# Hybrid decoder trunk, two layers on one core: sums and turns moved from TensorE to VectorE and DRAM, some low halves of weights to GpSimd

## The chip, the cores and the metric

The kernel runs on one NeuronCore of one Trainium2 chip. The metric is the device time of one execution in microseconds (us), median of several runs; lower is better. TensorE does the matrix products (in the profile PE, its weight loads PEld), VectorE is DVE, ScalarE is ACT, GpSimd is POOL, and SyncE (SP) issues DMAs. SBUF is the on-chip memory with 128 partitions, PSUM the banks into which TensorE writes, DRAM the memory outside the core.

## The reference

Two layers over a sequence of 512 tokens with 1024 features. One layer, cut to what matters here:

```
hn = rmsnorm(x, pre_g)
proj = hn @ w_in                       # 1024 x 6664
y_ret = retention(q, k, v) * silu(g)   # 4 heads, each head's output normalized over its 128 features
y_ssd = ssd_mixer(...)                 # 2 groups; values x * delta, states, rmsnorm over 256 features of a group
y_sb  = stick_breaking(...) * silu(g)  # 4 heads
y_mem = memory_read(q, rmsnorm(mem)) * silu(g)   # 4 heads
y = concat(y_ret, y_ssd, y_sb, y_mem) @ w_out    # 2048 x 1024
x = x + rmsnorm(y, post_g)
```

All of it is in float32.

## The kernel before, in words

**Products in three parts.** A float32 product is made of three matmuls in a shorter format. Each operand is split into a high half (ScalarE copies it into the short format, `split`, L293) and a low half (VectorE subtracts that copy from the original, L294), and `mm3` adds high times high, high times low and low times high (L287 to L290, all issued by `mm`, L285). Activations `hTh`, `hTl` hold the normalized input with features on partitions; weights `wh`, `wl` are 1024 columns wide and come in "subs".

**Weights.** A layer has 39 blocks of weights, each of two subs. Blocks come from DRAM in order into one of two `raw` buffers by a DMA that ScalarE's queue issues (L353). `w_prefetch` (L312) splits sub after sub into five slots of `wh` and `wl`: the split of sub k+5 can start when TensorE has finished with sub k. When the second sub of a block has been split, its `raw` buffer is free, and the DMA of the block after next is issued.

**Order.** The builder runs the layer once in Python, and a scheduler places each engine's instructions in an order of its own by a timeline; dependences, not the text, set it. Each projection counts as a unit (`tick`), and `defer(n, f)` runs `f` n units later, so that its operands have had time to arrive. A layer goes: memory values and keys, stick-breaking heads, retention heads, two state-space groups, gates, output projection in two halves of 512 columns (`out_proj`). At the layer change the second half's four token chunks (128 tokens each) end one after the other; `post` (L1164) makes the new x, stores it to DRAM, and `prenorm` (L484) normalizes it for the next layer and turns it, so that features lie on partitions: eight transposes of 128x128 on TensorE into PSUM (`transposed`, L479), then `split` into `hTh` and `hTl`. While chunks 1 to 3 end, TensorE already makes the next layer's memory keys and values; `behind` keeps each chunk's transposes after a given product. The next layer's first products of `hTh` are those of `sb_v` (`proj_a`, chunk after chunk, first the first four blocks of 128 features for all chunks, then the last four).

**Squares of a row.** The retention heads and the state-space groups need, for each token, a sum of squares over partitions. VectorE adds partitions 64 to 127 to 0 to 63 (and in the heads 32 to 63 to 0 to 31), the rest is split into high and low in `z`, and one matmul with a matrix of ones (`onesr`, L881 for two heads, L1069 for a group) adds up the partitions. `row_rstd` (L803) copies the resulting row to SBUF (L808), spreads it by DMA over 32 partitions of 16 tokens each (L811), GpSimd adds epsilon and takes the power -1/2 (L812, L813), and the result goes by DMA to DRAM (L815) and back, the same row into all partitions (L818). `scaled` (L886) and `ssd_norm` (L1075) multiply by it.

**State-space values.** `ssd_values` (L994) turns the two convolved tiles of a group by eight TensorE transposes (L1003) into PSUM and multiplies them from there by `delta` (L1007) and by the decay (L1009) for `ssd_states` and `ssd_out`.

**Turns by VectorE and DRAM** are already used for other tiles: `nc.vector.transpose` turns each 32x32 block in its place, four DMAs write the blocks to a buffer in DRAM, each to the place where it belongs (`through_dram`, L650; `columns_turned`, L663), and one DMA reads the turned tile back (L651, L668).

**GpSimd** already makes some low halves, those of the turned attention weights (L675, L759), and masks (L736, L835, L989).

## Time and profile before

| | |
|---|---|
| runs before | 923.71, 925.14, 924.06 us; median 924.06 us |
| profiled execution | 923.25 us; span of its instructions 921.5 us, so 1.75 us lie outside the span |
| mean granted TensorE clock in it | 0.998 |
| busy share: PE, PEld, DVE, ACT, POOL | 99%, 84%, 73%, 48%, 16% |
| instructions | 12952 |

How to read it: a busy share is the time in which at least one instruction of the engine was under way, over the span. Matmuls overlap in the pipeline: the duration of one (about 0.39 us at 512 columns) is longer than the time from its start to the next one's start, and it is the latter that TensorE's time is made of. A row of the timeline gives start, duration, engine, line, operation, tiles and count, and in brackets how long the engine sat idle before it and for whom. A line such as L285 is that of a helper; tiles (`wl`, `hTh`, `pj`, `mx`) say what it worked on. `pj` and `mx` are PSUM banks, `s`, `y`, `r` are SBUF tiles of 512 columns, `turned` and `row` buffers in DRAM.

### The profile page before, as it was taken

Reading aid. Unit: us, or ns where it says so; the run is one execution under the profiler, and the core shown is the slowest. Engines: PE = TensorE matmul, PEld = TensorE weight load, DVE = VectorE, ACT = ScalarE, POOL = GpSimd, SP = SyncE. Lnnn points to the kernel's source line nnn. Section 1 sums busy time; section 2 is a strip of 40 time slices with the busy share of each in tenths; the row PEclk is TensorE's granted clock in tenths of the full one; section 3 lists DMA queues with packets and bytes.
Section 4 is the critical chain, followed back from the end, with each engine's and each line's share of the span. In section 5 each row is a group of like instructions: output and inputs, shape, how many; then the busy total and the mean of one; then the engine's idle time right before and its main releaser. Section 6 shows DMA issues by size and latency. Waiting matters only on the chain.

```text
span 921.5 us, 12952 instructions
## 1 busy us (share of the span) xinstructions
PE 913.2 (99%) x4667; PEld 773.6 (84%) x4667; DVE 673.3 (73%) x1081; ACT 443.5 (48%) x841; POOL 146.3 (16%) x208
## 2 busy tenths in 40 slices
PE   9999999999999999999999999999999999999997
PEld 7998888888888888888899888888888888888885
DVE  6855689888787887844587476898778869687343
ACT  6643485744453342733465336675445434335341
POOL 1200152320131110100040002423112120102001
PEclk9999999999999999999999999999999999999999
DMA  8544664642444333444345256556333362422502
GB/s 316 213 141 144 169 167 104 199 146 61 120 134 148 116 109 126 137 149 158 116 173 196 93 172 183 124 122 183 103 109 116 110 194 92 139 95 88 210 12 91
DMA packets 105408, 128.53 MB, mean 139 GB/s; under 512 B 64640, under 2 KB 79744, under 8 KB 96256
## 3 DMA queue, kind: packets, MB, share of 16 engines
q10 hardware_dynamic: 10224, 73.44, 23.4%
q1 hardware_dynamic: 95120, 54.28, 20.7%
q8 instruction: 36, 0.59, 0.3%
q14 instruction: 28, 0.23, 0.1%
HBM read 112.10 MB, written 15.56 MB: 139 GB/s over the span
## 4 chain that ended last, share of the span: by engine, by line
PE 98%; DMA 1%; ACT 0%; DVEq 0%; SPq 0%; POOLq 0%; issue 0%; POOL 0%; ACTq 0%; DVE 0%
PE pj L285 74%; PE mx L285 23%; PE mx L479 1%; DMA mem<-memT 1%; PE mx L1003 0%; ACT s L523 0%; DVEq L1331 0%; ACT s L1168 0%; POOLq L1331 0%; ACT wh L293 0%; SPq L506 0%; SPq L349 0%; SPq L1206 0%; POOL t L449 0%; ACTq L1331 0%
## 5 line engine op out<-in xcount | busy, mean ns | idle before, releaser
L285 PE MATMUL pj<-hTh,wh 128*128 128x512 f32 x704 | 276.4, 393 | 0.0
L285 PE MATMUL pj<-hTh,wl 128*128 128x512 f32 x704 | 275.8, 392 | 0.0
L285 PE MATMUL pj<-hTl,wh 128*128 128x512 f32 x704 | 274.6, 390 | 0.0
L294 DVE TENSOR_TENSOR wl<-raw,wh 128x1024 fp32r<-128x1024 f32 (+2 forms) x156 | 188.6, 1214 | 116.9 <-ACT wh L293 115.7
L293 ACT CAST wh<-raw 128x1024 fp32r<-128x1024 f32 (+2 forms) x156 | 158.7, 1020 | 205.0 <-PE pj L285 177.5
L285 PEld LDWEIGHTS pj<-hTh,wl 128*128 128x128 f32 x704 | 132.2, 188 | 27.3
L285 PEld LDWEIGHTS pj<-hTh,wh 128*128 128x128 f32 x704 | 132.3, 188 | 27.1 <-DVE s L593 0.8
L285 PEld LDWEIGHTS pj<-hTl,wh 128*128 128x128 f32 x704 | 132.3, 188 | 26.6
L285 PE MATMUL pj<-wh,s 128*128 128x512 f32 x320 | 97.6, 391 | 0.0
L285 PE MATMUL mx<-s,s 128*128 128x256 f32 (+4 forms) x528 | 79.7, 307 | 0.0
L285 PE MATMUL mx<-wh,s 128*128 128x512 f32 x256 | 79.2, 389 | 0.0
L285 PEld LDWEIGHTS mx<-s,s 128*128 128x128 f32 (+1 forms) x528 | 65.8, 177 | 8.2 <-PE pj L285 1.4
L285 PEld LDWEIGHTS pj<-wh,s 128*128 128x128 f32 x320 | 59.7, 188 | 12.4
L285 PE MATMUL pj<-wl,s 128*128 128x512 f32 x160 | 60.2, 389 | 0.0
L285 PEld LDWEIGHTS mx<-wh,s 128*128 128x128 f32 x256 | 48.1, 188 | 10.0
L294 DVE TENSOR_TENSOR s<-y,s 128x512 fp32r<-128x512 f32 x64 | 41.2, 687 | 19.7 <-ACT s L293 14.0
L262 ACT ACTIVATE s<-s 128x128 f32<-128x128 f32 (+3 forms) x96 | 41.8, 478 | 22.3 <-DVE s L733 20.6
L675 POOL TENSOR_TENSOR s<-y,s 128x512 fp32r<-128x512 f32 x16 | 23.7, 1494 | 179.9 <-ACT s L674 179.4
L293 ACT CAST s<-y 128x512 fp32r<-128x512 f32 x64 | 36.6, 617 | 30.8 <-PE mx L285 22.0
L285 PE MATMUL mx<-wl,s 128*128 128x512 f32 x128 | 49.6, 389 | 0.0
L285 PE MATMUL pj<-wl,hTh 128*128 128x256 f32 (+2 forms) x144 | 47.6, 331 | 0.0
L285 PE MATMUL pj<-wh,hTl 128*128 128x256 f32 (+2 forms) x144 | 47.5, 330 | 0.0
(185 smaller groups left out, 1298.5 us busy)
## 6 DMA issues: line engine op xcount, KB each, us to landing
raw<-wts ACTq DMA_DIRECT2D x69, 1024.0 KB, 4.8
s<-x SPq DMA_DIRECT2D x24, 256.0 KB, 4.1
y<-turned SPq DMA_DIRECT2D x24, 256.0 KB, 2.8
turned<-y SPq DMA_DIRECT2D x64, 64.0 KB, 2.2
s<-acs SPq DMA_DIRECT2D x16, 256.0 KB, 6.3
r<-row SPq DMA_DIRECT2D x12, 256.0 KB, 5.0
raw<-wts SPq DMA_DIRECT2D x4, 512.0 KB, 7.5
raw<-wts SPq DMA_DIRECT2D x2, 1024.0 KB, 6.3
```

Of the source, the lines that this page charges most:

```text
L262: i = self.nc.scalar.activation(out, in_, func, **k)
L285: return self.nc.tensor.matmul(out, lhsT, rhs, start=start, stop=stop)
L293: self.nc.scalar.copy(h, src)
L294: self.nc.vector.tensor_sub(l, src, hf)
L479: x = self.nc.tensor.transpose(b[:, P * j:P * j + P], hn[i][:, P * j:P * j + P], self.con("ident", P))
L675: nc.gpsimd.tensor_sub(p.l, x, p.hf)
```

## The change

1. **Row sums.** The retention heads and state-space groups add partitions on VectorE down to 32; `row_rstd` then turns the 32 partitions by VectorE's transpose and sums over what were partitions by a `tensor_reduce`. The split of `z`, the matmul with `onesr`, the copy of the row and the DMA that spread it are gone. Since the 32 partitions now hold every 32nd token, the write of the row to DRAM goes token by token (pieces of one float) where it was 16 tokens at a time. `scaled` comes 6 units after the second head's squares (before: 3, then 7 more); `ssd_var` and `ssd_norm` each come one unit later.
2. **State-space values** are turned by `columns_turned` (VectorE's transpose, eight DMAs to DRAM, two back) straight after the convolution, and `ssd_values`, three units later instead of two, multiplies the read tiles in place.
3. **Layer change.** Chunk 0 of the new x is turned by `turned_far`: two transposes on VectorE, eight DMAs to DRAM, two back, then `split`. Chunks 1 to 3 stay on TensorE.
4. **Low halves.** `low_by_pool(k)` gives every third sub's low half to GpSimd, except in the memory and stick-breaking heads (subs 16 to 33 of a layer) and at the start: 36 of 156.

```diff
     def w_prefetch(self, upto=None, between=()):
...
-                self.split(x, h[:, c], l[:, c], h[:, c].bitcast(F32))
+                nc = self.nc
+                nc.scalar.copy(h[:, c], x)
+                (nc.gpsimd if self.low_by_pool(k) else nc.vector).tensor_sub(l[:, c], x, h[:, c].bitcast(F32))
...
+    def low_by_pool(self, k):
+        return k > 12 and k % 3 == 2 and not 16 <= k % (2 * NBLK) < 34
...
+    def turned_far(self, hn, t):
+        ts = slice(P * t, P * t + P)
+        H, HF, L = v3(self.hTh[:], KC), v3(self.hTh[:].bitcast(F32), KC), v3(self.hTl[:], KC)
+        for i in range(2):
+            T, ks = self.buf(tag=LT), slice(4 * i, 4 * i + 4)
+            self.nc.vector.transpose(T, hn[i])
+            d = self.turned_rows(SEQ, P)
+            dd = d.rearrange("(b m) (a t) -> a m b t", m=BLK, a=P // BLK)
+            x = self.through_dram(T, dd, d.rearrange("(k p) t -> p k t", p=P), v3(self.buf(tag=LL), 4))
+            self.split(x, H[:, ks, ts], L[:, ks, ts], HF[:, ks, ts])
...
     def row_rstd(...):
-        e = self.buf(tag="r")[0:n]
-        nc.scalar.copy(e, rows)
-        c = self.tiny(RJ)[:n * RP]
-        for i in range(n):
-            nc.sync.dma_start(c[RP * i:RP * i + RP], e[i:i + 1].rearrange("o (p j) -> o p j", j=RJ))
+        T, c = self.buf(tag=RT)[:n * RP], self.tiny(RJ)[:n * RP]
+        nc.vector.transpose(T, z)
+        nc.vector.tensor_reduce(out=c, in_=v3(T, RJ), op=ALU.add, axis=AX.X)
...
-        nc.sync.dma_start(d.rearrange("o (p j) -> (o p) j", j=RJ), c)
+        for i in range(n):
+            nc.sync.dma_start(d[i:i + 1].rearrange("o (j p) -> (o p) j", p=RP), c[RP * i:RP * i + RP])
...
     def ret_head2(...):
-        for n in (64, 32):
-            nc.vector.tensor_add(sq[0:n], sq[0:n], sq[n:2 * n])
...
-        nc.scalar.copy(z[r:r + 32], sq[0:32])
-        nc.vector.tensor_sub(z[r + 32:r + 64], sq[0:32], z[r:r + 32].bitcast(F32))
+        nc.vector.tensor_add(sq[0:64], sq[0:64], sq[64:128])
+        nc.vector.tensor_add(z[RP * (h % 2):RP * (h % 2) + RP], sq[0:32], sq[32:64])
...
-        vb = self.mx()[0:2]
-        self.mm(vb, self.onesr[:, 2:4], z[:], True, True)
...
     def ssd_group(...):
+        X["xt"] = [self.buf(tag=TX), self.buf(tag=TX)]
+        self.columns_turned(X["x"], X["xt"])
+        self.defer(VD, self.ssd_values, X)
-        self.defer(2, self.ssd_values, X)
...
     def ssd_values(...):
-            b = self.mx()
-            for c in (2 * i, 2 * i + 1):
-                for j in range(2):
-                    o = 256 * (c % 2) + P * j
-                    nc.tensor.transpose(b[:, o:o + P], X["x"][j][:, P * c:P * c + P], self.con("ident", P))
-            xdt, xds = self.buf(), self.buf()
+            b = xdt = X["xt"][i]
+            xds = self.buf()
...
     def ssd_var(...):
-        z = self.new(512, F32R, "r")
-        nc.scalar.copy(z[0:64], sq[1][0:64])
-        nc.vector.tensor_sub(z[64:128], sq[1][0:64], z[0:64].bitcast(F32))
-        row = self.mx()[0:1]
-        self.mm(row, self.onesr[:, 0:1], z[:], True, True)
-        X["rB"], = self.row_rstd(row, self.eps4[:RP])
+        nc.vector.tensor_add(sq[0][0:32], sq[1][0:32], sq[1][32:64])
+        X["rB"], = self.row_rstd(sq[0][0:32], self.eps4[:RP])
...
     def post(...):
-            self.turn.append(self.prenorm(x, preB, t))
+            self.turn.append((self.turned_far if t < FAR else self.turned)(self.normed(x, preB), t))
```

Here `VD` is 3, `RD` 6, `FAR` 1; `LT`, `LL` and `RT`, `TX` only name the kind of SBUF tile.

**What stands where.** ScalarE at the layer change. `s_4642` and `s_4636` are junk tiles of chunk 3's sum of squares, `y_4729` and `y_4723` memory keys, `raw_4852` and `raw_4846` the block with sub 90, the first after the four narrow subs of the first `proj_a`. Before:

```order
L293 CAST hTh<-mx_4561 128x4x128
L293 CAST wh_4848<-raw_4697 128x528
L462 ACTIVATE s_4642,t_4641<-s_4336 128x512
L462 ACTIVATE s_4643,t_4641<-s_4337 128x512
L293 CAST wh_4854<-raw_4762 128x528
L353 DMA raw_4852<-wts 128x2048
L293 CAST y_4729<-s_4727 128x512
L293 CAST hTh<-mx_4606 128x4x128
L293 CAST hTh<-mx_4613 128x4x128
```

And now, `y_4492` being the second half of chunk 0 that comes back from DRAM:

```order
L470 ACTIVATE s_4637,t_4635<-s_4323 128x512
L330 CAST wh_4842<-raw_4691 128x528
L295 CAST y_4723<-s_4721 128x512
L330 CAST wh_4848<-raw_4756 128x528
L295 CAST hTh<-y_4492 128x4x128
L295 CAST hTh<-mx_4600 128x4x128
L295 CAST y_4788<-s_4786 128x512
L295 CAST hTh<-mx_4607 128x4x128
L330 CAST wh_4852<-raw_4756 128x528
L361 DMA raw_4846<-wts 128x2048
```

The cast of chunk 0's second half now stands ahead of those of chunk 2 (`mx_4600`, `mx_4607`, before `mx_4606`, `mx_4613`), and the DMA of the block with sub 90, which stood ahead of them all, behind them.

SyncE at the layer change, where the new x is stored (`x_4542` is chunk 1's, `x_4594` chunk 2's, `x_4640` chunk 3's). Before:

```order
L1179 DMA x_4542<-s_4329 128x512
L1179 DMA x_4594<-s_4332 128x512
L1179 DMA x_4594<-s_4333 128x512
L1179 DMA x_4640<-s_4336 128x512
L1179 DMA x_4640<-s_4337 128x512
```

Now, with chunk 0's two halves written to `turned_4480` and `turned_4491` and read back:

```order
L1183 DMA x_4536<-s_4315 128x512
L667 DMA turned_4480<-y_4478 32x16x32 x4
L1183 DMA x_4588<-s_4318 128x512
L668 DMA y_4481<-turned_4480 128x4x128
L1183 DMA x_4588<-s_4319 128x512
L667 DMA turned_4491<-y_4489 32x16x32 x4
L1183 DMA x_4634<-s_4322 128x512
L1183 DMA x_4634<-s_4323 128x512
L668 DMA y_4492<-turned_4491 128x4x128
```

The read of chunk 0's first half stands behind a store of chunk 2, and that of its second half behind both stores of chunk 3.

VectorE in the first state-space group of layer 0, around the values. Before (`s_2898` is the second convolved tile, `mx_2964` and `mx_2975` the banks with the turned values):

```order
L943 SCALAR_TENSOR_TENSOR s_2898<-s_2898,s_2897 128x512
L294 TENSOR_TENSOR s_2726<-mx_2905,s_2726 128x128
L294 TENSOR_TENSOR wl_2955<-raw_2681,wh_2954 128x1024
L951 SCALAR_TENSOR_TENSOR s_2960<-s_2960,pj_2929 128x512
L1082 SCALAR_TENSOR_TENSOR y_1316<-y_1316,s_2960 128x512
L1007 TENSOR_TENSOR s_2969<-mx_2964,t_695 128x256 x2
L1009 TENSOR_TENSOR s_2970<-s_2969,t_713 128x256
```

Now (`s_2886` is that convolved tile, `s_2893` and `s_2894` the values read back, `s_3011` the convolution of the tile after it):

```order
L951 SCALAR_TENSOR_TENSOR s_2886<-s_2886,s_2885 128x512
L677 STREAM_TRANSPOSE y_2902<-s_2886 128x512
L894 TENSOR_TENSOR y_2214<-y_2214,r_2579 128x512
L894 TENSOR_TENSOR y_2376<-y_2376,r_2580 128x512
L331 TENSOR_TENSOR wl_2973<-raw_2686,wh_2972 128x1024
L296 TENSOR_TENSOR s_2731<-mx_2912,s_2731 128x128
L959 SCALAR_TENSOR_TENSOR s_2978<-s_2978,pj_2947 128x512
L1084 SCALAR_TENSOR_TENSOR y_1312<-y_1312,s_2978 128x512
L948 SCALAR_TENSOR_TENSOR s_3011<-pj_2982,hp_721,s_3011 128x511
L948 SCALAR_TENSOR_TENSOR s_3011<-pj_2982,hp_721,s_3011 128x510
L1013 TENSOR_TENSOR s_2893<-s_2893,t_691 128x256 x2
```

The multiplications by `delta` (L1013, before L1007) have moved behind the first two steps of the next convolution, and the normalization of retention heads 0 and 1 (L894, before L886) now stands ahead of them.

33 lines of the change are left out of this document (15 added, 18 removed).

## Prediction

> **What bounds the kernel now.** I read the page's busy shares and its chain first, then TensorE's list of waits, then the chain in order of time.
>
> ```profile
> span 921.5 us, 12952 instructions
> PE 913.2 (99%) x4667; PEld 773.6 (84%) x4667; DVE 673.3 (73%) x1081; ACT 443.5 (48%) x841; POOL 146.3 (16%) x208
> PE 98%; DMA 1%; ACT 0%; DVEq 0%; SPq 0%; POOLq 0%; issue 0%; POOL 0%; ACTq 0%; DVE 0%
> ...
> PE mx L285 <- POOL b L197: 1.2, 1, 1.2
> PE pj L285 <- ACT s L523: 1.0, 2, 0.7
> ...
> ACT wh L293 <- PE pj L285: 177.5, 84, 6.1
> 131.83 5.47 PE pj L285 x24
> ```
>
> A busy PE alone would prove little, since matmuls overlap; but the chain that ended last is 98% PE, and PE waited for others 2.2 us in all (1.2 and 1.0, both at the start). So everything that reaches TensorE is there in time, and the span is the sum of TensorE's issue intervals: 24 matmuls of 512 columns take 5.47 us, 0.228 each. The wait of ScalarE's `wh` casts for PE (177.5 us in all) says the same from the other side: a weight's split starts as soon as TensorE lets go of a slot, with four subs still ahead, 4 x 5.47 = 21.9 us where a sub is 24 such matmuls. An instruction less on TensorE is therefore time off the end, unless a new wait appears; an instruction more elsewhere costs nothing until it comes later than its slack.
>
> **What leaves TensorE.** The groups by shape, then three places of TensorE's timeline.
>
> ```profile
> L479 PE MATMUL mx<-consts,s 128*128 128x128 f32 x64 | 8.6, 273 | 0.0
> L1003 PE MATMUL mx<-consts,s 128*128 128x128 f32 x32 | 5.1, 272 | 0.0
> L285 PE MATMUL mx<-r,onesr 128*1 128x512 f32 x4 | 1.6, 398 | 0.0
> L285 PE MATMUL mx<-r,onesr 128*2 128x512 f32 x4 | 1.6, 396 | 0.0
> ...
> 484.80 1.03 PE L479 MATMUL mx<-consts,s 128*128 128x128 f32 x8
> 485.59 0.71 PE L285 MATMUL pj<-wh,s 128*128 128x512 f32 x2
> 486.14 0.39 PE L285 MATMUL pj<-wl,s 128*128 128x512 f32 x1
> ...
> 831.43 0.40 PE L285 MATMUL mx<-r,onesr 128*1 128x512 f32 x1
> 831.67 1.08 PE L285 MATMUL pj<-wh,s 128*128 128x512 f32 x4
> ```
>
> The 32 transposes L1003 go, 8 of the 64 L479 (chunk 0 of the layer change) and the 8 `onesr` matmuls. Their mean durations (272, 396 ns) are not their price, because they overlap with their neighbours. From 484.80 to 486.14 stand eight transposes and two ordinary matmuls: 1.34 - 2 x 0.228 = 0.88 us, 0.11 each. A `onesr` matmul takes 831.67 - 831.43 = 0.24. So 40 x 0.11 + 8 x 0.24 = 4.4 + 1.9 = **6.3 us** leave the stream. No instruction is added to it. The same rows give an uncertainty: after the eight transposes the next two matmuls took 0.55 instead of 0.46, so a switch between shapes costs 0.09. The scheduler regroups small products in the new order; ten switches more or fewer would be 0.9 us either way, and I take none.
>
> **What is added to VectorE and GpSimd.**
>
> ```profile
> L294 DVE TENSOR_TENSOR wl<-raw,wh 128x1024 fp32r<-128x1024 f32 x144 | 180.5, 1257 | 111.5 <-ACT wh L293 110.4
> L745 DVE STREAM_TRANSPOSE s<-s 128x512 f32<-128x512 f32 x8 | 5.5, 689 | 3.3 <-POOL s L736 3.3
> ...
> L294 DVE TENSOR_TENSOR wl<-raw,wh x156: 681/1225/1809, 5.3 to 897.9; 128x1024 fp32r<-128x1024 f32 x144, 128x528 fp32r<-128x528 f32 x8, 128x512 fp32r<-128x512 f32 x4
> L675 POOL TENSOR_TENSOR s<-y,s x16: 1285/1298/2285, 108.6 to 587.9; 128x512 fp32r<-128x512 f32 x16
> 124.30 4.13 POOL L675 TENSOR_TENSOR s<-y,s 128x512 fp32r<-128x512 f32 x2 [0.82 <-ACT s L674]
> 125.47 1.81 DVE L294 TENSOR_TENSOR wl<-raw,wh 128x1024 fp32r<-128x1024 f32 x1
> ...
> raw<-wts ACTq DMA_DIRECT2D x69, 1024.0 KB, 4.8
> ```
>
> VectorE loses 36 low halves (34 of 1024 columns at 1.26, two of 528 at 0.7: 44 us) and gains eighteen transposes and eight reductions, each 0.69 at most (a reduction taken like a transpose of 512 columns): 18 us. The subtractions of `z` that it also loses are not counted. It goes down by some 26 us out of 673 and, being waited for nowhere by TensorE, gives nothing to the time. GpSimd shows no 1024-column low half; two of 512 columns took 2 x 1.29 = 2.6 us alone and 4.1 beside VectorE (row 124.30), so one costs 2.6 to 4.6 us, 36 of them 94 to 166 us on an engine busy 146 of 921. Such a half arrives 2.6 to 4.6 us after its cast instead of about 1.3, out of 21.9 us of lead: nothing, as long as the lead stands. Behind it in GpSimd's queue stand masks and powers, whose readers come units (5.47 us each) later. When it is the second of a block, ScalarE's DMA of a later block waits for it, some 3 us longer than before, ahead of the casts queued there; that block's cast is due three subs (16.4 us) later and the load takes 4.8, so this too stays inside.
>
> The port between the two engines: in row 125.47 a VectorE low half beside GpSimd took 1.81, the longest of 156, against a median of 1.23, so GpSimd's work cost it 0.58 at most. The Trainium skill ("SBUF — State Buffer", Who interferes with whom) says that a VectorE operation with two SBUF inputs and a GpSimd operation that reads SBUF lock one another out for the whole instruction. By that VectorE would stand still for up to 36 x 2.6 = 94 us, an estimate from the GpSimd row; the trace bears out a conflict but not that length, since 1.81 is less than one operation of each. I take 0.58.
>
> **State-space values through DRAM.**
>
> ```profile
> 269.43 0.69 DVE L943 SCALAR_TENSOR_TENSOR s<-s,s 128x512 f32<-128x512 f32 x1 [0.76 <-ACT s L267]
> 273.46 0.76 DVE L1007 TENSOR_TENSOR s<-mx,t 128x256 f32<-128x256 f32 x2 [0.37 <-PE mx L1003]
> 278.48 1.52 DVE L940 SCALAR_TENSOR_TENSOR s<-pj,hp,s 128x511 f32<-128x511 f32 x2
> 298.80 2.35 PE L285 MATMUL mx<-s,s 128*128 128x128 f32 x14
> ...
> L663 SPq DMA_DIRECT2D turned<-y x48: 303/451/1466, 195.5 to 789.5; - x48
> DMA to landing us min/median/max: 1.5/2.9/5.7
> ...
> L651 SPq DMA_DIRECT2D y<-turned x16: 337/338/341, 82.2 to 576.7; - x16
> DMA to landing us min/median/max: 2.6/2.9/5.6
> ```
>
> In the first group the second convolved tile is done at 270.1. Add a transpose (0.7), four issues on SyncE (4 x 0.45 = 1.8), landing 2.9, the read's issue and landing 0.4 + 2.9: 278.8, with the slowest landings 284.3. The multiplications now stand behind two steps of the next convolution, which ran from 278.48 to 280.0. So VectorE waits 0 to about 4 us there, with that convolution and a low half queued behind it; the products that need the values come in the small matmuls that PE reached no earlier than 298.80. Cost taken: nothing; cover: 15 us.
>
> **Row sums.** The gather and the copy go, the transpose and reduction come (1.4 us), the row is written in single floats.
>
> ```profile
> 843.12 0.34 SPq L818 DMA_DIRECT2D r<-row  x1
> 846.60 1.41 DVE L1075 SCALAR_TENSOR_TENSOR y<-y,consts,r 128x512 f32<-128x512 f32 x2 [4.92 <-DMA r<-row]
> 871.80 0.39 PE L285 MATMUL mx<-wh,s 128*128 128x512 f32 x1
> ```
>
> The tightest reader is the last group's normalization: it gave the operands of the last two of sixteen steps of the output projection's first half, which ended at 871.80; a step is 12 x 0.228 = 2.7 us, so they were due at about 866.3 and split by about 849.5 (846.60 + 1.41 and two splits): 17 us of cover. One unit later takes 5.5 of it. A row is now 512 pieces; the nearest row, L663 with 256 pieces, lands after 2.9, at most 5.7, so 6 us more at the slow end. Cost taken: nothing. The Trainium skill ("DMA: Bandwidth & Descriptors", Rules for kernel authors) says that a non-contiguous last dimension becomes one descriptor per element and advises against it; no run here shows such a write yet, and by that rule too the price is latency in that cover.
>
> **The layer change** is where it is narrow.
>
> ```profile
> 471.00:488.00 17.00, 17.00 (x102) 14.85 (x101) 16.13 (x25) 11.39 (x26) 7.75 (x13) 1.00 0.50 177
> 463.83 19.95 SPq L1179 DMA_DIRECT2D x<-s  x8
> 487.96 0.28 PE L285 MATMUL pj<-wh,hTh 128*128 128x264 f32 x1
> 500.67 12.22 PE pj L285 x99
> ```
>
> In the clock of before, the last store of the new x was issued at 483.8; the read of chunk 0's second half now follows it, so it lands at 484.2 + 2.9 = 487.1, at the slow end 489.8. ScalarE casts it, and behind that wait chunk 2's casts and the DMA of the block with sub 90. Three deadlines follow; TensorE comes to each 0.9 us earlier, since chunk 0's transposes are gone.
> - Chunk 2's first half: landing + two casts (0.6 each) + up to two low halves (0.7 each) = 489.7 (slow 492.4). From 487.96 to 500.67 stand 96 matmuls and eight transposes, 0.123 each without the latter; TensorE needs it at 487.96 + 24 x 0.123 + 0.9 - 0.9 = 490.9. Slack 1.2, or a wait of 1.5.
> - Chunk 0's second half: landing + 0.6 + 0.7 = 488.4 (slow 491.1); needed after 48 of the matmuls, 487.96 + 5.9 = 493.9. Slack 5.5 or 2.8.
> - Sub 90: DMA some 3 us after the landing, 490.1; + 4.8 + cast 1.05 + low half 1.3 = 497.2 (slow 499.9); needed at 500.67 - 0.9 = 499.8. Slack 2.6, or 0.1 late.
>
> VectorE was busy 16.13 of 17.00 us from 471 to 488; it gains two transposes (1.4), loses a low half of 1024 and two of 528 columns (2.7), and beside GpSimd may lose 3 x 0.58 = 1.7: 16.5. It fits. Between a cost of 0 and 1.5 us I take 0, from the median landing.
>
> **Sum.** 923.25 - 6.3 = 916.95 for the profiled execution (1.75 us outside the span unchanged). The median of the runs stands 0.81 above it: **917.8 us**, 0.7% faster. A measurement can tell about 0.2% (1.85 us) from no change. Own range of this case: ten switches less (0.9) and the spread of the runs below (0.35) give 916.5; ten switches more and the wait of 1.5 give 920.2.
>
> **Rivals.** For the first, the landings of all DMAs with `turned`.
>
> ```profile
> L748 SPq DMA_DIRECT2D turned<-s x128: 302/449/2547, 128.1 to 637.8; - x128
> ...
> DMA to landing us min/median/max: 1.4/2.4/7.8
> ```
>
> - *The layer change waits.* The read lands later than 5.6 us after its issue: of all DMAs to and from `turned`, one took 7.8. Then (484.2 + 7.8 + 2.6) chunk 2 comes at 494.6, 3.7 us late, and 917.8 + 3.7 = 921.5. For it: narrow slack and a queue of stores ahead; against it: the landing median. 0.12.
> - *The port lock.* By whole-instruction locking, three low halves on GpSimd hold VectorE for 2.6 + 1.3 + 1.3 = 5.2 us in that stretch: 16.13 + 1.4 - 2.7 + 5.2 = 20.0 of 17, chunks 2 and 3 are 3 us late, 920.8. Against: 1.81. This is the rule of the Trainium skill's SBUF page named above. 0.03.
> - *Slower: weights come late.* A low half stands in GpSimd's in-order queue, and for 17 of the 36 the next load, in ScalarE's queue, stands behind it. If such a half were done more than 16.4 - 4.8 + 21.9 - 2.3 = 31 us after its cast, every microsecond beyond costs TensorE 17 us in all: 917.8 + 17 = 935 at 32 us; slower by 0.2% is reached at about 31.5. For it: GpSimd waits there for tiles that come late (masks, powers); against: the longest of its subtractions took 2.3 us, and the lead is ten times that. 0.06.
> - *No change.* TensorE only looks like the pace, and weight loads or ScalarE take over what it gives back: 924.1. Against: waits of 2.2 us. 0.05.
>
> **How the numbers follow.** Forecast 0.74. Faster: 0.74 + 0.12 + 0.03 = 0.89; same: 0.05; slower: 0.06. The range takes the forecast's own and most of the waiting layer change: 916.5 to 920.8.
>
> **What would show it.** After: no L1003-like transposes, 56 left of the others, no `onesr`; PE's waits still about 2 us; the layer's units as long as before. A row "PE pj <- ACT hTh" or "<- DVE hTl" near 485 would be the first rival, VectorE low halves of over 2 us the second, "PE <- POOL wl" the third. I am wrong if the span is above 919 with PE waiting, or if PE waits nowhere and yet less than 5 us are gone.

## The result: slower by 5%, and the profile after

The changed kernel takes 968.87 us (median of 4 runs, 967.91 to 970.29); the kernel before took 923.89 us (4 runs, 923.71 to 925.14) beside it. The ratio is 1.0497 [1.0485, 1.051]. The forecast was 917.8 us with 920.8 as the upper end.

The page of the changed kernel: its span, the busy time of each engine, and the chain that ended last by engine and by line.

```profile
span 968.6 us, 12904 instructions
PE 927.7 (96%) x4619; PEld 780.9 (81%) x4619; DVE 662.9 (68%) x1060; ACT 430.6 (44%) x821; POOL 241.5 (25%) x244
PE 67%; DMA 12%; DVE 11%; ACT 4%; POOL 3%; issue 3%; SPq 1%; DVEq 0%; ACTq 0%; POOLq 0%
PE pj L287 48%; PE mx L287 18%; DMA row<-t 4%; DMA s<-acs 3%; DMA raw<-wts 2%; POOL t L828 2%; DVE wl L331 2%; DMA r<-row 1%; DVE s L1026 1%; ACT wh L330 1%; DVE s L948 1%; DVE s L998 1%; DVE s L296 1%; DVE y L894 1%; ACT s L264 1%
```

The chain was 98% TensorE; now a third of it lies elsewhere, and the lines named are those of the new rows: the row's write (`row<-t`), the power ahead of it (L828), the row's read, and the broadcasts of the state-space sums (`s<-acs`). VectorE's busy time fell by 10.4 us, where the sum had 26. TensorE's own account: it stood idle for 968.6 - 927.7 = 40.9 us instead of 921.5 - 913.2 = 8.3, which is 32.6 more; and it was busy 14.5 us longer although it has 48 instructions less. The granted clock shows why (mean 0.978 after, 0.998 before): added up over stretches of one microsecond, a lower clock took 17.5 us of TensorE's busy time, and none in the kernel before.

Some of the waits of the changed kernel (engine, line, what it waited for: us in total, times, longest):

```profile
DVE y L1077 <- DMA r<-row: 45.0, 4, 13.5
...
DVE s L998 <- DMA s<-acs: 40.3, 4, 12.0
...
PE mx L287 <- DVE s L1039: 9.4, 3, 4.8
...
PE mx L287 <- DMA s<-turned: 7.4, 4, 2.2
PE mx L287 <- ACT s L295: 6.8, 3, 3.9
```

TensorE's own waits add up to some 34 us. Of these 2.3 us stand at the start, as before, and nearly all the others between 262 and 428 us and between 740 and 861 us, in and just behind the state-space groups of the two layers. VectorE waited 85 us in front of two kinds of DMA, in eight waits of 10 to 11 us on average. The kernel before has the same two waits, with 19.1 us in all:

```profile
DVE y L1075 <- DMA r<-row: 13.9, 4, 4.9
...
DVE s L988 <- DMA s<-acs: 5.2, 6, 2.3
```

Everything that VectorE would have done meanwhile (convolutions, the mixing of the decays, low halves) came late, and TensorE then waited for some of that. The first such place, from SyncE's timeline (start, length of the issue, line, what is issued) and VectorE's:

```profile
250.79 0.84 SPq L831 DMA_DIRECT2D row<-t  x2
256.73 0.34 SPq L834 DMA_DIRECT2D r<-row  x1
257.31 0.38 SPq L685 DMA_DIRECT2D s<-turned  x1
...
258.29 2.62 SPq L996 DMA_DIRECT2D s<-acs  x4
```

```profile
253.87 0.69 DVE L1084 SCALAR_TENSOR_TENSOR y<-y,s 128x512 f32<-128x512 f32 x1
266.60 1.40 DVE L998 TENSOR_TENSOR s<-s,t 128x512 f32<-128x512 f32 x2 [12.04 <-DMA s<-acs]
```

SyncE issues in order. The row is written at 250.79, its read waits on SyncE until the write has landed, at 256.73, and behind that read stand a turned read that TensorE needs and the four broadcasts of the first decay. These go out at 258.29, the first lands 8.3 us later, and VectorE does nothing from 254.56 to 266.60. TensorE, for its part, waits 2.2 us for the turned read, until 262.79. The same place in the kernel before:

```profile
250.98 1.84 SPq L986 DMA_DIRECT2D s<-acs  x4
265.47 1.24 SPq L811 DMA_DIRECT2D t<-r  x2
271.21 0.49 SPq L815 DMA_DIRECT2D row<-t  x1
272.95 0.80 SPq L818 DMA_DIRECT2D r<-row  x2
```

There the broadcasts went first and landed after 4.0 to 6.4 us, and the row's write (271.21) was followed by its read 1.7 us later. In the changed kernel the four broadcasts took 8.2 to 8.6 us to land: they now ran beside the row's two reads and a 1 MB load of weights issued at 257.94, and the DMA engines were 90% busy or more from 260 to 266. So several things are new at once: where the row stands in the queue, how long its write takes to land, and what the DMAs behind it share the engines with. The experiments vary the first two. All row writes before, then all after (issues, and us from issue to landing):

```profile
L815 SPq DMA_DIRECT2D row<-t x8: 316/403/493, 271.2 to 840.4; - x8
DMA to landing us min/median/max: 1.7/2.2/5.4
```

```profile
L831 SPq DMA_DIRECT2D row<-t x12: 302/306/496, 250.8 to 887.1; - x12
DMA to landing us min/median/max: 5.8/6.5/7.4
```

Written float by float, the rows take 6.5 us instead of 2.2 to land (medians; in the kernel before, the two rows of a pair of heads went in one DMA). The chain in order of time shows two more places, at a group's norm and at the layer change:

```profile
363.70 1.40 POOL t L828
365.12 6.58 DMA row<-t
371.72 3.53 DMA r<-row
375.94 0.75 DVE y L1077
376.69 2.39 DVE s L1026 x4
...
505.15 4.19 DMA turned<-y
509.49 2.48 DMA y<-turned
```

That the chain passes through the layer change does not make it a loss: TensorE waited nowhere there for more than 0.1 us.

### The profile page after: what moved, and what is told of

The parts are those of the page before. It is cut to its first block, busy times and chain, and to the rows that moved or that the text cites. A ratio compares the mean times of both kernels' runs of the same rounds, so it can differ in the third digit from the quotient of the medians.

```text
span 968.6 us, 12904 instructions
## 1 busy us (share of the span) xinstructions
PE 927.7 (96%) x4619; PEld 780.9 (81%) x4619; DVE 662.9 (68%) x1060; ACT 430.6 (44%) x821; POOL 241.5 (25%) x244
## 2 busy tenths in 40 slices
DMA packets 135009, 133.76 MB, mean 138 GB/s; under 512 B 91168, under 2 KB 109344, under 8 KB 125856
## 4 chain that ended last, share of the span: by engine, by line
PE 67%; DMA 12%; DVE 11%; ACT 4%; POOL 3%; issue 3%; SPq 1%; DVEq 0%; ACTq 0%; POOLq 0%
PE pj L287 48%; PE mx L287 18%; DMA row<-t 4%; DMA s<-acs 3%; DMA raw<-wts 2%; POOL t L828 2%; DVE wl L331 2%; DMA r<-row 1%; DVE s L1026 1%; ACT wh L330 1%; DVE s L948 1%; DVE s L998 1%; DVE s L296 1%; DVE y L894 1%; ACT s L264 1%
## 5 line engine op out<-in xcount | busy, mean ns | idle before, releaser
L287 PE MATMUL pj<-hTl,wh 128*128 128x512 f32 x704 | 277.8, 395 | 0.0
L331 DVE TENSOR_TENSOR wl<-raw,wh 128x1024 fp32r<-128x1024 f32 (+2 forms) x120 | 146.1, 1223 | 82.4 <-ACT wh L330 68.7
L331 POOL TENSOR_TENSOR wl<-raw,wh 128x1024 fp32r<-128x1024 f32 (+1 forms) x36 | 89.4, 2482 | 284.3 <-ACT wh L330 284.2
L287 PEld LDWEIGHTS pj<-hTh,wh 128*128 128x128 f32 x704 | 134.5, 191 | 27.9 <-DVE s L610 0.8
L287 PE MATMUL mx<-s,s 128*128 128x256 f32 (+4 forms) x528 | 91.5, 340 | 24.6 <-DVE s L1039 9.4
L287 PEld LDWEIGHTS mx<-s,s 128*128 128x128 f32 (+1 forms) x528 | 73.0, 196 | 37.7 <-issue 12.5
L296 DVE TENSOR_TENSOR s<-y,s 128x512 fp32r<-128x512 f32 x64 | 48.3, 800 | 19.5 <-ACT s L295 15.8
```

What stands on the lines that cost most here:

```text
L287: return self.nc.tensor.matmul(out, lhsT, rhs, start=start, stop=stop)
L296: self.nc.vector.tensor_sub(l, src, hf)
L331: (nc.gpsimd if self.low_by_pool(k) else nc.vector).tensor_sub(l[:, c], x, h[:, c].bitcast(F32))
```

## The experiments

The theories, as they are named in the expectations: R, the new row sums cost (R1 by the 4-byte pieces of their write, R2 by their earlier place on SyncE); V, the values through DRAM; G, the low halves on GpSimd; Q and D, whether a late row acts through SyncE's queue or through its own readers. Each kernel was timed beside the kernel before; the ratio to it stands with its interval.

**Undoing the row sums, or making them alone.** `e1_rows_as_before` puts back `row_rstd`, `ret_head3`, `onesr` and `ssd_var`'s split of before into the changed kernel.

```diff
+        vb = self.mx()[0:2]
+        self.mm(vb, self.onesr[:, 2:4], z[:], True, True)
...
-            nc.sync.dma_start(d[i:i + 1].rearrange("o (j p) -> (o p) j", p=RP), c[RP * i:RP * i + RP])
+        nc.sync.dma_start(d.rearrange("o (p j) -> (o p) j", j=RJ), c)
```

> The changed kernel with the row sums as they were before (z split into two, one matmul by onesr, gather, row written in pieces of 64 bytes); low halves on GpSimd, values through DRAM, the far turn and the later norms stay. Theory R (the new row sums are what costs: their row write lands 6 to 7 us after its issue, and the reads and broadcasts behind it on SyncE come late): the loss goes and 40 transposes are saved, 923.9 - 4.4 = 919.5 us. Rival V (the values through DRAM or the low halves on GpSimd starve VectorE): it stays above 950 us.

Measured: 951.68 us, 1.0308 [1.0291, 1.0325]. The loss is not gone; V's figure holds. The wait has moved to the values:

```profile
DVE s L1023 <- DMA s<-turned: 29.6, 4, 10.9
```

`e4_rows_alone` makes the opposite kernel: before, with the new `row_rstd`, the new `ret_head2` and `ssd_var`, and nothing else.

```diff
-            self.defer(3, self.ret_head3, h // 2, z, ys)
+            i = h // 2
+            self.defer(RD, self.scaled, ys, self.row_rstd(z, self.con("reps", 2 * RJ, 2 * RP)[:, RJ * i:RJ * i + RJ], 2))
```

> The kernel before with the new row sums alone (turn and reduction on VectorE, write in pieces of 4 bytes, use six units after the squares; group norms at their old distance); no other part of the change. Theory R: it is slow by itself, over 940 us. Rival V: the row sums alone save the eight onesr matmuls, 923.9 - 1.9 = 922 us.

Measured: 957.11 us, 1.0367 [1.0348, 1.0386]. R's figure holds: the row sums alone cost 34 us. With `e1` this says that neither part is innocent, and that their costs don't add up.

**The size of the pieces.** In `e2_rows_in_64b` the last addition stores its sums so that token 16p+j, not 32j+p, ends in row p; the write then has 16 floats in a piece, and the constant is laid out as before.

```diff
-        nc.vector.tensor_add(z[RP * (h % 2):RP * (h % 2) + RP], sq[0:32], sq[32:64])
+        self.add_by_row(z[RP * (h % 2):RP * (h % 2) + RP], sq[0:32], sq[32:64])
...
+    def add_by_row(self, out, a, b):
+        a, b = (x.rearrange("q (p j) -> q p j", j=RJ) for x in (a, b))
+        self.nc.vector.tensor_add(out.rearrange("q (j p) -> q p j", p=RP), a, b)
...
-            nc.sync.dma_start(d[i:i + 1].rearrange("o (j p) -> (o p) j", p=RP), c[RP * i:RP * i + RP])
+            nc.sync.dma_start(d[i:i + 1].rearrange("o (p j) -> (o p) j", j=RJ), c[RP * i:RP * i + RP])
```

> The changed kernel, but token 16p+j instead of 32j+p ends in row p, place j of the reduced tile, because the last addition writes its sums in that order; the row is then written in pieces of 64 bytes instead of 4. Instructions and their number stay. Theory R1 (the size of the pieces): the write lands 1.7 to 3.4 us after its issue instead of 5.9 to 7.0; about 4.4 us less at each of the eight rows, all of which the chain passes through or nearly: 8 x 4.4 = 35 us, about 934 us. Rival R2 (the place in SyncE's queue: the row's write and read stand ahead of the decay's broadcasts, and wait for the power on GpSimd): the landing is shorter but the wait stands, not below 950 us.

Measured: 930.06 us, 1.0075 [1.0046, 1.0103]. R1: 39 of the 45 us are gone, with as many instructions on every engine as in the changed kernel, on SyncE and GpSimd in the same order and on the others in nearly the same. The write, and the two waits:

```profile
L835 SPq DMA_DIRECT2D row<-t x12: 312/318/421, 251.5 to 840.5; - x12
DMA to landing us min/median/max: 1.3/1.4/3.0
```

```profile
DVE y L1081 <- DMA r<-row: 16.3, 4, 5.1
...
DVE s L1002 <- DMA s<-acs: 9.2, 4, 4.5
```

**The place.** `e3_rows_later` keeps the 4-byte pieces and issues the turn, sums, power, write and reads three units later.

```diff
-            self.defer(RD, self.scaled, ys, self.row_rstd(z, self.con("reps", 2 * RJ, 2 * RP)[:, RJ * i:RJ * i + RJ], 2))
+            self.defer(3, self.rows_late, i, z, ys)
...
+        self.defer(7, self.scaled, ys, self.row_rstd(z, self.con("reps", 2 * RJ, 2 * RP)[:, RJ * i:RJ * i + RJ], 2))
```

> The changed kernel, with the turn, reduction, power, write and read of a pair of retention rows issued three units later and their use one unit later, as far from the squares as before; the write is still in pieces of 4 bytes. Theory R2 (the place in the queue): the first decay's broadcasts go ahead of the first pair's write again, so the first of the three places in each layer (about 8 to 10 us) is made good, about 950 us. Theory R1 (the size of the pieces): the writes still land 6 to 7 us after their issue and what stands behind them is only another victim, above 960 us.

Measured: 982.59 us, 1.064 [1.0608, 1.0671]: 14 us slower than the changed kernel, which neither theory had (R1's bound alone holds). The broadcasts' wait fell from 40.3 to 20.6 us, but the values' reads now stand behind the row, and VectorE's wait for them rose from 4.0 to 28.8 us. Moving the row only changed what stands behind it.

The next three kernels, together with `e4`, make a square of piece size and distance on the kernel before, with the row sums alone. `e11_rows64_alone` has 64-byte pieces (the edit of `e2`) at the old distances (the edit of `e3`).

> The kernel before with the new row sums alone, in pieces of 64 bytes and at the old distances (three units, then seven). Theory R1: nothing is late and the eight onesr matmuls are saved, 923.0 - 1.9 = 921.1 us, against 957.1 for the row sums alone in pieces of 4 bytes. Rival: the turn and reduction on VectorE or the removed hop do harm by themselves, over 925 us.

Measured: 920.68 us, 0.9978 [0.9969, 0.9987]: as forecast by R1, and faster than both kernels. `e13_rows4_old_distance` is the same with the write, its constant and the last additions of the change:

```diff
-            nc.sync.dma_start(d[i:i + 1].rearrange("o (p j) -> (o p) j", j=RJ), c[RP * i:RP * i + RP])
+            nc.sync.dma_start(d[i:i + 1].rearrange("o (j p) -> (o p) j", p=RP), c[RP * i:RP * i + RP])
```

> The kernel before with the new row sums alone at the old distances (three units, then seven), the write in pieces of 4 bytes: it differs from the kernel that took 920.7 us in the size of the pieces alone. Theory R1 (the landing of the write): it lands 6.5 us or later instead of 1.4 and the kernel takes over 940 us. Rival P (the distances decide; at the old ones the 5 us more are covered): 921 to 925 us.

Measured: 936.3 us, 1.0145 [1.0128, 1.0161], landing 6.2/7.5/8.5. The bound of 940 was missed, yet the pieces alone cost 15.6 us at the old distances. `e17_rows64_short_alone` takes `e4_rows_alone` and applies the edit of `e2`.

> The kernel before with the new row sums alone, pieces of 64 bytes, at the new distance (write and reads three units earlier on the queues, use six units after the squares). It fills the square of piece size and distance: 957.1 (4 bytes, new distance), 936.3 (4 bytes, old), 920.7 (64 bytes, old). Theory P3 (the two costs add up, and the earlier place also costs with short landings, since the row's write and reads stand ahead of the decay's broadcasts): 928 to 932 us, which is the 7 to 9 us left in the change with pieces of 64 bytes. Rival (the distance matters only where the write lands late): 920 to 922 us.

Measured: 923.35 us, 1.0003 [0.9993, 1.0012]. P3 falls; the rival is right in kind, and its 922 is missed by 1.4 us. The square is:

| row sums alone | old distance | new distance |
|---|---|---|
| pieces of 64 bytes | 920.7 | 923.4 |
| pieces of 4 bytes | 936.3 | 957.1 |

The new distance costs 2.7 us with a short landing and 20.8 with a long one; the pieces cost 15.6 and 33.8. Taken singly they cost 2.7 and 15.6 us, together 36.4: each makes the other dearer. The new distance changes two places at once, since the row's write and reads go out three units earlier on SyncE and the row is used four units earlier on VectorE; the square does not tell these apart. The next two kernels try to.

**Which way the late row acts.** Both kernels keep the 4-byte pieces. `e9_rows_on_gpsimd` issues the row's write and reads from GpSimd's queue, `e10_acs_on_scalar` the broadcasts from ScalarE's.

```diff
-            nc.sync.dma_start(d[i:i + 1].rearrange("o (j p) -> (o p) j", p=RP), c[RP * i:RP * i + RP])
+            nc.gpsimd.dma_start(d[i:i + 1].rearrange("o (j p) -> (o p) j", p=RP), c[RP * i:RP * i + RP])
...
-            nc.sync.dma_start(out[i], d[i:i + 1].to_broadcast([P, SEQ]))
+            nc.gpsimd.dma_start(out[i], d[i:i + 1].to_broadcast([P, SEQ]))
```

> The changed kernel, its rows still written in pieces of 4 bytes, but the row's write and the reads of it issued by GpSimd (which made the power) instead of SyncE. Theory Q (the loss is SyncE's one queue: while it waits for the row's landing, the decay's broadcasts and the reads behind it are not issued): VectorE's waits for those broadcasts (40 us) shrink and the time falls by 20 us or more, below 950 us. Theory D (the row itself comes late to its two readers on VectorE, whichever queue carries it): the landing stays 6 to 7 us and the time stays above 960 us.

Measured: 978.64 us, 1.06 [1.0585, 1.0614], by its time for D. But it isn't a clean test. VectorE's wait for the broadcasts did fall, to 11.1 us, and the wait moved to GpSimd, whose masks then held TensorE:

```profile
POOL r L834 <- DMA row<-t: 33.5, 6, 7.4
...
PE mx L287 <- POOL s L851: 11.7, 4, 5.9
```

```diff
-            nc.sync.dma_start(v3(a, 4), S["rows"][0, r:r + 4].unsqueeze(0).to_broadcast([P, 4, P]))
+            nc.scalar.dma_start(v3(a, 4), S["rows"][0, r:r + 4].unsqueeze(0).to_broadcast([P, 4, P]))
...
-            nc.sync.dma_start(v3(E[64 * j:64 * j + 64], 4), S["rows"][1, r:r + 4].unsqueeze(0).to_broadcast([64, 4, P]))
+            nc.scalar.dma_start(v3(E[64 * j:64 * j + 64], 4), S["rows"][1, r:r + 4].unsqueeze(0).to_broadcast([64, 4, P]))
```

> The changed kernel with rows in pieces of 4 bytes, all still on SyncE, but the broadcasts of the state-space sums (the decay's and the outputs') issued by ScalarE. Theory Q: these broadcasts no longer stand behind the row's landing; of the three places in each layer at which the chain leaves TensorE, the two with a broadcast behind the row go or shrink: below 950 us. Theory D: the waits move to the row's own readers and the time stays above 960 us.

Measured: 955.8 us, 1.0361 [1.0327, 1.0395]: 13 us back, between the two bounds. VectorE's waits for the broadcasts fell from 40.3 to 18.7 us and for the row from 45.0 to 30.2. So part of the loss is what stood behind the row on SyncE, and a wait for the row itself remains. This test is not clean either: ScalarE's `wh` casts now waited 10.7 us for the row's landing, for which they did not wait before, so the 13 us are a net figure.

**The values through DRAM.** `e6_values_alone` adds them alone to the kernel before.

```diff
-        self.defer(2, self.ssd_values, X)
+        X["xt"] = [self.buf(tag="s"), self.buf(tag="s")]
+        self.columns_turned(X["x"], X["xt"])
+        self.defer(3, self.ssd_values, X)
...
-        self.defer(5, self.ssd_var, X)
-        self.defer(9, self.ssd_norm, X)
+        self.defer(6, self.ssd_var, X)
+        self.defer(10, self.ssd_norm, X)
```

> The kernel before with the state-space values through DRAM alone (taken three units after the convolution, group norms one unit later); row sums, low halves and layer change as before. Theory S (values and row hops share SyncE's one queue, so that the values' read is issued late and VectorE stands in front of it): it is slow by itself, 945 to 955 us. Rival G (the loss of the kernel with the old row sums came from the low halves on GpSimd): 32 transposes are saved, 922.9 - 3.5 = 919.4 us.

Measured: 946.44 us, 1.025 [1.0235, 1.0265]. S holds: by themselves they cost 23 us beside the old rows. VectorE waited 17.5 us in front of their reads. In the first group the last of their writes went out at 275.26, just behind the row's two reads (273.97) and a load of weights (272.85), and the values were read at 281.06. `e5_rows64_values_pe` takes `e2` and turns them on TensorE again (`defer(2, self.ssd_values, X)` and the transposes of before).

> The changed kernel with rows written in pieces of 64 bytes and, besides, the state-space values turned on TensorE as before (two units after the convolution); new row sums, low halves on GpSimd and the far turn stay. Theory S (what is left of the loss is VectorE waiting for the values' read, and everything behind it): the loss of 7 us goes, 8 transposes and 8 onesr matmuls stay saved: 922.9 - 0.9 - 1.9 = 920.1 us. Rival R2 (the row's write and read ahead of the decay's broadcasts cost by their place): not below 926 us.

Measured: 932.25 us, 1.0105 [1.0088, 1.0122]. S falls and R2's bound holds: beside the new rows with short landings the values cost nothing (930.06 with them). `e12_rows64_vd5` gives them more time in `e2`:

```diff
-VD = 3
+VD = 5
```

> The changed kernel with rows in pieces of 64 bytes and the state-space values taken five units after the convolution instead of three. Theory S: the wait of VectorE for the values' read (about 5 us in each layer's first group) goes: 923.0 - 6.3 plus what the rows' place still costs, 917 to 924 us. Rival: the wait is not what was left, 928 to 932 us.

Measured: 932.0 us, 1.0091 [1.0077, 1.0105]: the rival's figure. But the edit did not take the wait away: it was 3.5 us in `e2` and is 3.6 here. So this run does not test S; `e5`, where the wait does not exist, does. `e14_rows64_old_distance_all` has all parts, the edit of `e2` and the later rows of `e3`, so that the row's DMAs come between the values' writes.

> All parts of the changed kernel, rows in pieces of 64 bytes and at the old distances (three units, then seven). Theory P2 (the 7 us that are left with pieces of 64 bytes come from the row's write and read standing ahead of the decay's broadcasts): these waits go and it takes 917 to 922 us. Rival V2 (they come from the values through DRAM together with the rows on SyncE): with the row's hops now between the values' writes and their read as in the kernel with the old rows, it takes over 935 us.

Measured: 939.5 us, 1.0186 [1.0171, 1.02]: V2. Its SyncE timeline, and the landings of the values' writes issued from 268 to 271 and from 275.9 to 276.5:

```profile
268.53 1.96 SPq L680 DMA_DIRECT2D turned<-y  x4
272.71 0.79 SPq L835 DMA_DIRECT2D row<-t  x2
274.04 0.82 SPq L838 DMA_DIRECT2D r<-row  x2
274.95 2.52 SPq L680 DMA_DIRECT2D turned<-y  x4
284.92 0.90 SPq L685 DMA_DIRECT2D s<-turned  x2
```

```profile
L680 SPq DMA_DIRECT2D turned<-y x4: 318/498/512, 268.5 to 270.0; - x4
DMA to landing us min/median/max: 1.7/1.9/1.9
```

```profile
L680 SPq DMA_DIRECT2D turned<-y x2: 537/759/981, 275.9 to 276.5; - x2
DMA to landing us min/median/max: 7.3/7.8/8.3
```

The same 64 KB land after 1.9 us ahead of the row's two broadcast reads, and after up to 8.3 behind them, so the values are read at 284.92. The row's reads were not alone there: a 1 MB load of weights went out at 275.17, among these writes. `e18_row_reads_on_scalar` issues these reads from ScalarE instead.

```diff
-            nc.sync.dma_start(out[i], d[i:i + 1].to_broadcast([P, SEQ]))
+            nc.scalar.dma_start(out[i], d[i:i + 1].to_broadcast([P, SEQ]))
```

> All parts of the change with rows in pieces of 64 bytes at the old distances (939.5 us), but the two broadcast reads of each row issued by ScalarE. Theory B (the values' last write landed 8.3 us after its issue since it stands behind the two row broadcasts of 256 KB in SyncE's DMA queue): it lands after 2 to 3 us and the time falls below 932 us. Rival E (the 16 DMA engines are shared by all queues, so the broadcasts hold the write from any queue; or the wait is VectorE's own): the landing stays at 5 us or more and the time at 936 us or above.

Measured: 945.4 us, 1.0237 [1.022, 1.0255]. By its time E's bound holds; the landings are between the two: the writes behind the row now take 4.2 to 4.9 us and the values are read at 280.72, 4 us earlier. The load of weights came later too (278.02), so the run does not show how much of the 8.3 us was the row's reads and how much the load. The time is lost again on ScalarE, whose casts stand behind reads that wait for the row (15.4 and 12.2 us).

**Low halves and the far turn.** `e7_low_alone` is the kernel before with the new lines of `w_prefetch` and `low_by_pool`.

```diff
-                self.split(x, h[:, c], l[:, c], h[:, c].bitcast(F32))
+                nc = self.nc
+                nc.scalar.copy(h[:, c], x)
+                (nc.gpsimd if self.low_by_pool(k) else nc.vector).tensor_sub(l[:, c], x, h[:, c].bitcast(F32))
```

> The kernel before with the 36 low halves on GpSimd alone. Theory S: hidden, 922.9 us within 1. Rival G (they delay the powers and masks behind them and hold VectorE by the shared port): above 930 us.

Measured: 924.3 us, 1.0013 [1.0004, 1.0022]. G falls; the price is 1.3 us, a little over S's bound. `e8_rows64_low_dve` takes them from GpSimd again in `e2`:

```diff
-        return k > 12 and k % 3 == 2 and not 16 <= k % (2 * NBLK) < 34
+        return False
```

> The changed kernel with rows written in pieces of 64 bytes and all low halves on VectorE again; values through DRAM stay. Theory S: VectorE leads the chain behind the values' read, so eight to ten low halves of 1.2 us more in those stretches make it 10 us slower than the same kernel with them on GpSimd, about 940 us. Rival G: the low halves on GpSimd cost, so it is faster than that kernel's 930.1 us.

Measured: 929.73 us, 1.0069 [1.0054, 1.0084]. Neither: the same as `e2`'s 930.06. `e15_rows64_far_off` is `e2` with the far turn off (the edit below), and `e16_rows64_alone_far` is `e11` with it on:

```diff
-LT, LL, FAR = "y", "y", 1
+LT, LL, FAR = "y", "y", 0
```

> The changed kernel with rows in pieces of 64 bytes and the layer change's first chunk turned by TensorE again. By the forecast's account the far turn saves 0.9 us: 930.1 + 0.9 = 931 us. Rival (the far turn makes TensorE wait at the layer change, 1 to 2 us): 928 to 930 us.

Measured: 933.52 us, 1.011 [1.0088, 1.0131], nearer the forecast's account; its interval and that of `e2` overlap.

> The kernel before with the new row sums in pieces of 64 bytes at the old distances (920.7 us) and the far turn besides; low halves on VectorE and values on TensorE. By the forecast's account: 920.7 - 0.9 = 919.8 us. Rival (the far turn makes TensorE wait at the layer change): 921 to 923 us.

Measured: 922.74 us, 0.9992 [0.9981, 1.0003], the rival's figure: 2 us more than `e11` where 0.9 less was due. The eleven runs go from 919.96 to 924.78, and the interval just overlaps that of `e11`. TensorE has one new wait, at the layer change, in front of a bank that VectorE empties late:

```profile
488.19 0.36 PE L287 MATMUL pj<-wh,hTh 128*128 128x264 f32 x1 [2.27 <-DVE s L587]
```

The same wait stands in `e8` (2.29 us at 490.81), the other kernel in which VectorE makes all low halves and also turns chunk 0; in `e2`, with a third of the low halves on GpSimd, TensorE does not wait there. That would explain why the two tests point in opposite directions.

## Why the prediction was wrong

**What bounds the kernel: right.** TensorE was the pace, and an instruction less on it is time off the end when no wait takes its place: `e11` drops the eight `onesr` matmuls and gains 2.4 us (923.12 to 920.68), where 8 x 0.24 = 1.9 was forecast.

**What leaves TensorE: right in count; the size, 6.3 us, is not confirmed.** The changed trace has 56 of the transposes of x left and no `onesr` matmul. In `e2`, without the 3.1 us that a lower clock took, TensorE's busy time is 4.7 us below that of the kernel before (911.6 - 3.1 and 913.2). In the changed kernel TensorE got such a gain and gave back more as waits (some 32 us) and lower clock (17.5 us): the sum counted its stream as if nothing else could set it.

**The row sums: the step that failed.** The prediction took "the nearest row, L663 with 256 pieces, lands after 2.9, at most 5.7, so 6 us more at the slow end. Cost taken: nothing." The landing itself was not far outside that: 5.8 to 7.4 us. What failed is "nothing", on three counts.
- The cover was read at one reader, the last group's norm, with 17 us. VectorE's in-order queue stood in front of all four norms for 45.0 us, and behind the first group's norm of each layer it held the decays' mixing (L1026) and the state updates, for which TensorE then waited.
- SyncE's in-order queue was not followed. The row sums are made at once instead of three units later, so the row's write and the reads that wait for its landing moved ahead of the first decay's broadcasts. The prediction neither priced that move nor named what stands behind it. In the trace these broadcasts went out at 258.29 instead of 250.98, and VectorE waited 12.0 us there, some of it because they also took longer to land.
- The two were taken as separate small latencies. The square shows that their costs don't add up: 2.7 us for the distance with a short landing, 20.8 with a long one.

Of the rules weighed in the prediction, the Trainium skill's on the last dimension ("DMA: Bandwidth & Descriptors", Rules for kernel authors) was the better guide. The packets under 512 B bear it out: 91168 in the changed kernel and 85408 in `e2`, and the difference of 5760 is 12 rows x (512 - 32) pieces. Each float was a packet of its own. "By that rule too the price is latency in that cover" was the wrong conclusion from it.

**State-space values: right in size, wrong as a zero.** VectorE waited 4.0 us for them in the changed kernel, within the 0 to 4 forecast. It did not hold where the row's reads came between their writes: by themselves, beside the old rows, they cost 23 us (`e6`). The landing of 2.9 was taken for a queue without the row's broadcasts; behind these, and beside a load of weights, it was up to 8.3 (`e14`).

**Low halves: right that they are hidden.** 1.3 us alone (`e7`), nothing in `e8`. Their size on GpSimd was 2.5 us, below the 2.6 to 4.6. The port's price was wrong: I took 0.58 us from the longest of 156 low halves. In `e7` VectorE's busy time fell by 9.7 us (673.3 to 663.6), where the low halves taken from it are 44 us by the prediction: the rest of its work took some 34 us longer, 0.95 for each low half. In the changed kernel a subtraction of 0.69 took 2.48 (445.46), and at the layer change an update of 0.75 took 2.9:

```profile
492.70 3.56 DVE L1176 SCALAR_TENSOR_TENSOR s<-s,t,s 128x512 f32<-128x512 f32 x2
```

```profile
492.50 2.55 POOL L331 TENSOR_TENSOR wl<-raw,wh 128x1024 fp32r<-128x1024 f32 x1
```

The pair that takes 1.41 elsewhere took 3.56 beside one GpSimd low half. The Trainium skill's rule ("SBUF — State Buffer", Who interferes with whom), a lock for the whole instruction, agrees with this; the prediction had set it aside. TensorE has no wait at the layer change, so these two rows cost no time; in `e2` a longer one does (below).

**The layer change: 0 taken, and 0 in the changed kernel.** The half's write landed after 4.19 us and the read after 2.48 (the last two rows of the chain above), and a load of weights stands behind them in the chain; but all came in time, and TensorE waited there 0.1 us at most. Added to `e11`, where VectorE keeps its low halves, the far turn cost 2.1 us instead of saving 0.9 (`e16`), with a wait of 2.27 us for VectorE; that load of VectorE is a case that the prediction did not have to meet.

**The rivals.** The one on the slower side blamed GpSimd's queue and late weights; TensorE's list of waits names no weight. The mechanism is there in small, though: the chain passes twice from a GpSimd low half to the load that stands behind it, here in layer 1; by themselves the low halves cost 1.3 us (`e7`).

```profile
652.41 2.44 POOL wl L331
...
655.32 8.28 DMA raw<-wts
```

The chance of 0.06 for slower was too small because that rival was the only mechanism looked for on that side: no rival was built from the two in-order queues that the change moved instructions in.

**What stays open.** With pieces of 64 bytes the whole change still takes 930 us where the parts' own prices would give less. Low halves 1.3, the far turn 2.1 and the distance 2.7, each measured alone, come to 6.1; on 920.7 that is 926.8, and the values' 32 transposes (3.5 us) should come off it. The profiled execution of `e2` (927.78 us) shows where the rest is: after the start TensorE waits twice, once in each layer, 3.00 and 3.26 us for the first step of a convolution (L952), and the second of these waits is followed by a stretch of half clock that takes 3.1 us. The first place, from VectorE's timeline and TensorE's:

```profile
290.58 5.51 DVE L1019 TENSOR_TENSOR s<-s,t 128x256 f32<-128x256 f32 x3
298.46 0.47 PE L287 MATMUL pj<-hTh,wh 128*128 128x512 f32 x1 [3.00 <-DVE s L952]
```

Just ahead of that convolution stand the values' multiplications by the decay (L1019). The third of them took 4.8 us in each layer, where 0.42 is the rule, beside a row's power (289.48, 3.96 us) and a low half (293.43, 2.38 us) on GpSimd; without these 4.4 us the convolution would have come before TensorE needed it. With the low halves back on VectorE (`e8`) no such multiplication takes over 0.43 us, but waits of 2.3 us at the layer change and 4.3 us in the state-space groups stand in their place, and the time is the same. So no single undoing (`e5`, `e8`, `e12`, `e15`) brought the rest back; no run was made that removes both. How a late row divides between SyncE's queue and its own readers is shown only as far as `e10` goes, a net 13 of 45 us, and how much of the late landings is the load of weights beside them is open.

## What to carry to other kernels

A DMA whose landing an in-order queue must wait for delays everything that stands behind it there: list that, on the issuing engine and on the reader's, before calling a latency covered. Write short rows so that each piece is a run of many floats, here by letting an earlier instruction store its result in the order of the write, which cost no instruction and was worth 39 us. And a saving on the engine that sets the pace is kept only while no new wait is put in front of it: of the parts tried by themselves only the row sums with 64-byte pieces, at the old distances, gained (920.7 us).

## What the runs showed of the hardware

- A row of 2 KB written to DRAM in 512 pieces of 4 bytes landed after 5.8/6.5/7.4 us (min, median, max of twelve rows in the changed kernel), in 32 pieces of 64 bytes after 1.3/1.4/3.0 (twelve rows in `e2`).
- After some waits of 2 us or more TensorE ran on at half its clock, after others not. In the changed kernel the clock fell to 0.50 within 1.5 us after waits of 2.22 us (262.79), 2.07 (283.10), 1.98 (379.18) and 2.51 (857.63), and stayed there for 3 to 7 us; after 2.06 (309.22), and in other kernels after 2.27 (`e16`, 488.19) and 3.00 (`e2`, 298.46), it stayed at 1.00. Stretches around the first of these (length, then busy time of PE, PEld, DVE, ACT and POOL, then granted clock, DMA share, GB/s):

```profile
256.00:260.40 4.40, 4.40 (x23) 3.52 (x21) 0.00 (x0) 1.14 (x3) 1.85 (x1) 1.00 0.40 47
260.40:262.80 2.40, 0.18 (x2) 0.01 (x1) 0.00 (x0) 0.00 (x0) 0.00 (x0) 1.00 0.98 323
262.80:264.57 1.77, 1.77 (x12) 1.77 (x13) 0.00 (x0) 0.00 (x0) 0.00 (x0) 0.81 0.99 411
264.57:267.13 2.56, 2.56 (x7) 1.98 (x7) 0.53 (x1) 0.00 (x0) 0.00 (x0) 0.50 0.95 371
267.13:270.00 2.87, 2.87 (x14) 2.35 (x13) 2.86 (x5) 1.22 (x2) 2.02 (x3) 0.97 0.09 34
```

  From 264.57 on six matmuls took 0.43 us each instead of 0.23: this wait of 2.2 us cost another 1.2 or more. The Trainium skill ("TensorE: Matmul & The Clock Gate", What's actually happening) gives one idle window of about 3.4 us as what brings the half clock; here shorter gaps did, and not each time.
- In `e2` one VectorE multiplication of 128x256 in each layer, 0.42 us as a rule, took 4.8 us, beside a power of 3.96 or 3.95 us and a low half of 2.38 or 2.37 on GpSimd that followed one another.
